# Two long-convolution filters moved to the start of a two-block forward pass, with a transform that pairs frequencies

## Chip, cores, metric

One core of one Trainium2 chip. The metric is the device time of one execution in microseconds (us). Before the change the median of 3 runs is 1393.35 us (1392.62 to 1395.66).

## What is computed

Two blocks over 256 tokens of width 1024. The first has two layers. Each layer modulates a normalized x by vectors made from a condition (`ada_w`), multiplies it by a wide `w_in`, and runs three branches: differential attention, a gated convolution ("hyena") and a gated MLP. In layer 0 a second stream, the context, goes through the same steps; in layer 1 it serves as keys and values only. The second block is a sparse attention and a feed-forward part; the change does not touch it.

The hyena branch convolves `u = x1 * v` with a filter of the sequence's length. The filter depends on weights alone, not on x:

```
z    = [t, cos(bands*wpos), -sin(bands*wpos)]              # 256 x 33
hid  = sin(freq0 * (z   @ w1 + b1))                        # 256 x 64
hid  = sin(freq1 * (hid @ w2 + b2))                        # 256 x 64
h    = (hid @ w3).reshape(256, 2, 512) * exp(-t*deltas)    # forward and backward half
k    = concat(h[:, 0], 0, reversed h[1:, 1]) / norm
y    = irfft(rfft(u) * rfft(k))[:256] + u * bias
```

The kernel does not use an FFT. It multiplies by cosine and sine matrices at 256 odd half-frequencies: `eo[.,0]` (sum of both halves) with cosines gives `Kc`, `eo[.,1]` (difference) with sines gives `Ks`, and the squared sums give the norm `rr`.

## The kernel before, in words

One class, `Body`, emits the program; `run` makes the pools, `block1` and `block2` emit the blocks. Each weight chunk of 512 KB is loaded by SyncE's queue (SP) into a `raw` buffer (3 of them), rounded by ScalarE to `hi` (L81), and VectorE makes the residue `lo` (L82): `unit`. TensorE then does three products per tile, hi with the high part of x, hi with its low part, lo with the high part (L61). Products of the filter are plain fp32 and show as two instructions each.

`block1` starts with the modulation of layer 0: four `mod_chunk` calls, each with two loads of 1 MB, fp32 products, two small transposing products and a few VectorE steps that end in `modA`. x and the context are loaded, normalized, transposed by TensorE (L735), modulated (L741, L743) and split into `hTh` and `hTl`. As soon as a pair of 128-row blocks of `hT` is there, its part of the first product X1 runs; four such steps interleave with `mod_chunk` 1 to 3. Then come packB (constants) and `filter_load(0)`.

The loop over the layers calls `hyena_in` (the rest of X1, then HV and X0, each four units of weights per layer), `hyena_filter`, `hyena_core` (the convolution by `K`), `gmlp`, the attention and the three gated branches. In layer 0 both the load and the computing of the filter come in that order, and its first hidden layer is the only part that reaches the startup. In layer 1 `filter_load(1)` stands right ahead of `hyena_filter`.

`hyena_filter` has two hidden layers (a small product, L401, six VectorE steps of `sin_red`, a sine on ScalarE at L261), then for each half of the 256 times two expansions by `w3`, five VectorE steps (L412 to L418) and two squares, then 16 small instructions for the norm and 8 products by `CS` that ScalarE copies to `K` (L433).

The order on each engine's queue is not the program's order as it stands. A planner replays the program when it is built, with the priority of program order, estimated durations and the number of free buffers, and writes each engine's queue; on the chip a queue runs strictly in order and waits where an input is late. SP's queue holds all loads, and a load waits there for its buffer.

Buffers that matter here: `slab` (8 KB per partition, 10 of them, shared by almost every large tile), `tf` (3 scratch tiles of 2 KB), 4 PSUM banks `pm` for all products but the large ones, 4 banks `pg` for those, and `x1` (the output of block 1, unused until the end of layer 0).

Of the kernel before, what the change touches and what calls it, by code (L numbers as in the profile page):

```python
# [7 lines left out]
F32 = mybir.dt.float32  # L8
# [23 lines left out]
class Body:  # L32
# [9 lines left out]

    def pool(self, name, bufs, psum=False, ctx=None):
        kw = dict(space=PSUM) if psum else {}
        return (ctx or self.ctx).enter_context(self.tc.tile_pool(name=name, bufs=bufs, **kw))
# [323 lines left out]

    def filter_load(self, l):  # L370
        nc = self.nc
        f = self.filt
        s1, s2, s3, s4 = [self.slab(f"f{i}").rearrange("p a b -> p (a b)") for i in range(4)]
        w3 = s1[:64, 0:1024]
        sqs = s1[:, 1024:2048].rearrange("p (t c) -> p t c", t=2)
        eo = s2.rearrange("p (t i c) -> p t i c", t=2, i=2)
        CS = s3[:, 0:1024].rearrange("p (t i f) -> p t i f", t=2, i=2)
        dec = s3[:, 1024:2048].rearrange("p (t c) -> p t c", t=2)
        zT = s4[:33, 0:256]
        hs = [s4[:64, 256:512], s4[:64, 512:768]]  # L380
        w1, w2 = s4[:33, 768:832], s4[:64, 832:896]
        nc.sync.dma_start(zT, self.a["zT"])
        nc.sync.dma_start(w1, self.a["hy_f_w1"][l])
        nc.sync.dma_start(w2, self.a["hy_f_w2"][l])
        nc.sync.dma_start(w3, self.a["hy_f_w3"][l])
        nc.sync.dma_start(CS, self.a["dft_k"])
        nc.sync.dma_start(dec, self.a["decay"])
        fc = f.tile([64, 4], F32, name=self.nm("ffc"), tag="ffc")
        nc.sync.dma_start(fc, self.a["hy_f_cols"][l])
        return w1, w2, w3, zT, hs, fc, eo, CS, dec, sqs  # L390

    def hyena_filter(self, l, ld):
        nc = self.nc
        f = self.filt
        w1, w2, w3, zT, hs, fc, eo, CS, dec, sqs = ld
        src = zT
        for i, w in enumerate((w1, w2)):
            ps = self.bank()[:64, :256]
            self.mm(ps, w, src)
            h = hs[i]  # L400
            nc.vector.tensor_scalar(h, ps, fc[:, i:i + 1], fc[:, 2 + i:3 + i], op0=OP.add, op1=OP.mult)  # L401
            self.sin_red(h, h, 256, p=64)
            src = h
        nps = self.bank()
        tcol = self.load_const("t0mask", [128, 2], pool=f)
        for t in range(2):
            h0 = self.bank()
            h1 = self.bank()
            self.mm(h0, src[:, t * 128:t * 128 + 128], w3[:, :512])
            self.mm(h1, src[:, t * 128:t * 128 + 128], w3[:, 512:])  # L410
            a0, a1 = self.tf(), self.tf()
            nc.vector.tensor_tensor(a0, h0, dec[:, t], op=OP.mult)  # L412
            nc.vector.scalar_tensor_tensor(a1, h1, tcol[:, t:t + 1], dec[:, t], op0=OP.mult, op1=OP.mult)
            nc.vector.tensor_tensor(eo[:, t, 0], a0, a1, op=OP.add)
            nc.vector.tensor_tensor(eo[:, t, 1], a0, a1, op=OP.subtract)
            nc.scalar.activation(a0, a0, AF.Square)
            nc.scalar.activation(a1, a1, AF.Square)
            nc.vector.tensor_tensor(sqs[:, t], a0, a1, op=OP.add)  # L418
        for c in range(4):
            for t in range(2):  # L420
                self.mm(nps[:, 2 * c:2 * c + 2], sqs[:, t, c * 128:c * 128 + 128], self.ones[:, :2], t == 0, t == 1)
        ssq = self.col(4, "hss")
        nc.vector.tensor_copy(ssq, nps[:, :8].rearrange("p (c i) -> p c i", i=2)[:, :, 0])
        rr = f.tile([128, 4], F32, name=self.nm("rr"), tag="rr")
        self.rpow(rr, ssq)
        nc.vector.tensor_scalar(rr, rr, 1.0 / 512.0, None, op0=OP.mult)
        K = self.slab("hyK")
        for i in range(2):
            for fi in range(2):
                ps = self.bank()  # L430
                for t in range(2):
                    self.mm(ps, CS[:, t, i, fi * 128:fi * 128 + 128], eo[:, t, i], t == 0, t == 1)
                nc.scalar.copy(K[:, 2 * i + fi], ps)  # L433
        return K, rr

# [265 lines left out]
    def block1(self, x1):  # L701
        nc, a = self.nc, self.a
        self.mc = [self.c1.tile([128, 24, 2], F32, name=f"mc{l}") for l in range(2)]
        self.A = [self.c1.tile([128, 8, 2], F32, name=f"modA{l}") for l in range(2)]
        self.load_pack("packA", PACK_A, self.const)
        c1 = self.cin
        self.cs = self.c1.tile([128, 8, 32], F32, name="cs")
# [4 lines left out]
        nc.vector.tensor_tensor(self.cs[:, :, 0:2], c1, th, op=OP.mult)  # L712
        self.mod_chunk(0, 0)
        xin = [a["x"], a["ctx"]]
        xs = []
        for s in range(2):
            t = self.slab("xs").rearrange("p a b -> p (a b)").rearrange("p (t d) -> p t d", t=2)
            nc.sync.dma_start(t, xin[s].rearrange("(t p) d -> p t d", p=128))
            xs.append(t)
        for s in range(2):  # L720
            for t in range(2):
                r = self.row_rstd(xs[s][:, t])
                nc.vector.tensor_scalar(xs[s][:, t], xs[s][:, t], r, None, op0=OP.mult)
        hTh = self.hT.tile([128, 8, 512], F32R, name="hTh0", tag="hTh")
        hTl = self.hT.tile([128, 8, 512], F32R, name="hTl0", tag="hTl")
        x1b = [self.gbank() for _ in range(4)]
        op0 = lambda k: (hTh[:, k], hTl[:, k])
        for ch in range(4):
            un = self.unit(a["w_in"][0][W1CH["X1"]][ch], 2)
            for k in (2 * ch, 2 * ch + 1):  # L730
                ps = self.bank()
# [23 lines left out]
        for l in range(2):  # L755
# [10 lines left out]
            u, x0 = self.hyena_in(l, nst, op, [(b, f, 1) for f, b in enumerate(x1b)] if l == 0 else None)  # L766
            K, rr = self.hyena_filter(l, fl if l == 0 else self.filter_load(l))
            if l == 1:
                self.pc = self.flat("packC")
                self.load_pack("packC", PACK_C, self.pc)  # L770
                self.rope_tables()
# [500 lines left out]
    def run(self):  # L1272
        nc, P = self.nc, self.pool
        self.const = P("const", 1)
        self.c1 = P("c1", 1)
        self.filt = P("filt", 1)
        self.cols = P("cols", 3)
        self.scr = P("scr", 2)
        self.att = P("att", 2)
        self.hT = P("hT", 1)  # L1280
        self.wraw, self.whi, self.wlo = P("wraw", 3), P("whi", 4), P("wlo", 4)
        self.slabs = P("slabs", 10)
        self.psg, self.psm = P("psg", 4, True), P("psm", 4, True)
        self.ones = self.const.tile([128, 128], F32, name="ones")
        nc.vector.memset(self.ones, 1.0)
        self.mhalf = self.const.tile([128, 1], F32, name="mhalf")
        nc.vector.memset(self.mhalf, -0.5)
        x1 = self.const.tile([128, 2, 1024], F32, name="x1")
        hTp = self.block1(x1)
        self.block2(x1, hTp)  # L1290


def prepare(inp):
    import numpy as np

# [28 lines left out]
    g = {k: np.asarray(v) for k, v in inp.items()}  # L1324
    o = {}
# [19 lines left out]
    hyb = c(cols(g["hy_bias"], 4).transpose(2, 0, 1))  # L1345
    o["hy_f_w1"] = c(g["hy_f_w1"])
    o["hy_f_w2"] = c(g["hy_f_w2"])
    o["hy_f_w3"] = c(g["hy_f_w3"])
    o["hy_f_cols"] = c(np.stack([g["hy_f_b1"], g["hy_f_b2"], g["hy_f_freq"][:, 0], g["hy_f_freq"][:, 1]], axis=-1))
    o["gm_ln_g"] = c(g["gm_ln_g"])  # L1350
# [14 lines left out]
    fi = g["w_ffn_in_2"][0]  # L1365
    fo = np.concatenate([np.concatenate([r(j * 256, j * 256 + 256), 2816 + r(j * 256, j * 256 + 256)]) for j in range(11)])
# [29 lines left out]
    rr = np.arange(128)  # L1396
# [10 lines left out]
    tt = np.arange(256)  # L1407
    fo = np.concatenate([np.arange(0, 256, 2), np.arange(1, 256, 2)]) + 0.5
    ang = 2 * np.pi * tt[:, None] * fo[None] / 512.0
    o["dft_k"] = c(np.stack([np.cos(ang), np.sin(ang)], axis=1).astype(f32).reshape(2, 128, 2, 256)  # L1410
                   .transpose(1, 0, 2, 3))
    fh = fo.reshape(2, 128)
# [13 lines left out]
    z = np.concatenate([t, np.cos(bands * wpos), -np.sin(bands * wpos)], axis=-1).astype(f32)  # L1426
    o["zT"] = c(z.T)
    deltas = np.abs(np.linspace(math.log(1e-2) / 1.5, math.log(1e-2) / 0.3, 512, dtype=f32))
    o["decay"] = c(np.exp(-t * deltas).astype(f32).reshape(2, 128, 512).transpose(1, 0, 2))
    m = np.ones((128, 2), f32)  # L1430
    m[0, 0] = 0.0
    o["t0mask"] = m
    loc = locals()
# [19 lines left out]
```

## Time and profile before

| | |
|---|---|
| median of 3 runs | 1393.35 us |
| profiled execution | 1392.87 us |
| its span, first to last instruction | 1390.9 us |
| granted TensorE clock over the span | 1.00 |

Times in the profile are microseconds from the first instruction. A row of a timeline gives start, duration, engine, line, operation, output and inputs by the program's names, shapes, a count of merged instructions, and in brackets the idle time of that engine just before with what ended it. A row of a stretch gives its length, then the busy time of each engine with its number of instructions, the granted clock (1.00 is 2.4 GHz), the mean busy share of the 16 DMA engines and what they moved in GB/s. TensorE is PE (matmul) and PEld (weight load), VectorE DVE, ScalarE ACT, GpSimd POOL, and SPq is SyncE's queue. `f` is the name of the old filter's tiles (its scratch apart), `pm` of a PSUM bank.

### The profile page before, as it was taken

To read this page: it belongs to the slowest core of one execution; us is meant where nothing else is said; L and a number is where in the kernel's file an instruction comes from. 1 tells how busy PE (TensorE), PEld (TensorE's weight loads), DVE (VectorE), ACT (ScalarE), POOL (GpSimd) and SP (SyncE) were. 2 spreads that over 40 slices of the span, in tenths; PEclk is the share of its full clock that TensorE was granted. 3 is DMA by queue.
4 is the path that set the end of the run, shared out by engine and by line. 5 is a ranking of instruction groups with operands and counts; after the bars stand their busy time and mean duration, and the time that the engine had idled before them with its cause. 6 is when DMAs were issued, how large, how long until landed. Compare 5 with 4: busy or idle time off the path is not lost.

```text
span 1390.9 us, 19805 instructions
## 1 busy us (share of the span) xinstructions
PE 1355.7 (97%) x7721; PEld 1134.1 (82%) x7721; DVE 897.1 (64%) x1574; ACT 621.5 (45%) x1046; POOL 43.3 (3%) x55
## 2 busy tenths in 40 slices
PE   6999999999999999999999999999999999999998
PEld 3786888777888888788688899987878897899996
DVE  3757842685388977388856755667776567655545
ACT  3532432564332334375535644554554645444433
POOL 0000000000000000010000000001002000000000
PEclk9999999999999999999999999999999999999999
DMA  9431222112535545327334255558315356665551
GB/s 388 143 107 61 81 89 92 63 46 67 201 111 191 220 178 183 136 92 234 107 96 135 93 171 187 182 165 289 122 57 160 103 173 193 207 204 191 184 182 46
DMA packets 55261, 206.22 MB, mean 148 GB/s; under 512 B 7102, under 2 KB 8320, under 8 KB 51584
## 3 DMA queue, kind: packets, MB, share of 16 engines
q1 hardware_dynamic: 55168, 204.95, 43.6%
q8 instruction: 61, 1.00, 0.3%
q14 instruction: 32, 0.26, 0.1%
HBM read 203.37 MB, written 1.05 MB: 147 GB/s over the span
## 4 chain that ended last, share of the span: by engine, by line
PE 83%; DVE 7%; DMA 4%; ACT 3%; issue 2%; POOL 1%; SPq 0%; POOLq 0%; ACTq 0%; DVEq 0%
PE pg L61 67%; PE pm L61 13%; DVE lo L82 1%; DMA ada<-ada_w 1%; PE pm L243 1%; DMA f<-hy_f_w 1%; DMA raw<-w_in 1%; ACT hi L81 1%; PE pm L614 1%; DMA xs<-x 1%; ACT p L603 1%; PE pm L947 1%; DVE hTl L67 1%; POOL rstd L145 0%; DVE mx L599 0%
## 5 line engine op out<-in xcount | busy, mean ns | idle before, releaser
L82 DVE TENSOR_TENSOR lo<-raw,hi 128x1024 fp32r<-128x1024 f32 (+1 forms) x242 | 293.6, 1215 | 246.2 <-ACT hi L81 245.1
L81 ACT CAST hi<-raw 128x1024 fp32r<-128x1024 f32 (+1 forms) x242 | 252.1, 1044 | 385.4 <-PE pg L61 332.5
L61 PE MATMUL pg<-hTh,hi 128*128 128x256 f32 (+1 forms) x920 | 305.0, 333 | 1.8 <-DMA f<-hy_f_w 1.4
L61 PE MATMUL pg<-hTl,hi 128*128 128x256 f32 (+1 forms) x920 | 305.2, 332 | 1.1 <-DVE hTl L67 1.1
L61 PE MATMUL pg<-hTh,lo 128*128 128x256 f32 (+1 forms) x920 | 303.9, 331 | 0.3 <-DVE lo L82 0.3
L61 PEld LDWEIGHTS pg<-hTh,hi 128*128 128x128 f32 x920 | 174.0, 189 | 24.5 <-issue 4.2
L61 PEld LDWEIGHTS pg<-hTl,hi 128*128 128x128 f32 x920 | 174.2, 189 | 21.0 <-issue 4.3
L61 PEld LDWEIGHTS pg<-hTh,lo 128*128 128x128 f32 x920 | 174.1, 189 | 18.5 <-issue 2.8
L61 PE MATMUL pg<-lo,hTh 128*128 128x512 f32 x400 | 158.7, 397 | 0.5 <-DVE lo L82 0.5
L61 PE MATMUL pg<-hi,hTh 128*128 128x512 f32 x400 | 158.9, 397 | 0.3 <-ACT hTh L66 0.2
L61 PE MATMUL pg<-hi,hTl 128*128 128x512 f32 x400 | 157.5, 394 | 1.0 <-DVE hTl L67 1.0
L82 DVE TENSOR_TENSOR wsl<-raw,wsl 128x1024 fp32r<-128x1024 f32 x66 | 80.2, 1223 | 70.1 <-ACT wsl L81 69.4
L61 PE MATMUL pg<-hTh,wsl 128*128 128x256 f32 x576 | 105.2, 284 | 0.0
L81 ACT CAST wsl<-raw 128x1024 fp32r<-128x1024 f32 x66 | 68.4, 1048 | 80.3 <-PE pg L61 50.3
L61 PEld LDWEIGHTS pg<-hTh,wsl 128*128 128x128 f32 x576 | 90.5, 192 | 0.3
L61 PEld LDWEIGHTS pg<-hi,hTl 128*128 128x128 f32 x400 | 75.2, 188 | 18.1 <-DVE hTl L67 1.9
L61 PEld LDWEIGHTS pg<-lo,hTh 128*128 128x128 f32 x400 | 75.3, 188 | 17.8 <-issue 2.5
L61 PEld LDWEIGHTS pg<-hi,hTh 128*128 128x128 f32 x400 | 75.2, 188 | 17.4 <-issue 1.5
L61 PE MATMUL pg<-hTl,wsl 128*128 128x256 f32 x288 | 81.7, 284 | 0.0
L61 PE MATMUL pg<-gh,lo 128*128 128x512 f32 (+1 forms) x192 | 64.8, 337 | 0.0
L61 PE MATMUL pg<-gh,hi 128*128 128x512 f32 (+1 forms) x192 | 64.7, 337 | 0.0
L61 PE MATMUL pg<-gl,hi 128*128 128x512 f32 (+1 forms) x192 | 64.6, 337 | 0.0
(363 smaller groups left out, 2031.8 us busy)
## 6 DMA issues: line engine op xcount, KB each, us to landing
raw<-w_in SPq DMA_DIRECT2D x172, 512.0 KB, 3.6
raw<-w_ffn_in SPq DMA_DIRECT2D x36, 512.0 KB, 3.6
ada<-ada_wT SPq DMA_DIRECT2D x16, 1024.0 KB, 6.8
raw<-w_branch SPq DMA_DIRECT2D x24, 512.0 KB, 3.5
raw<-w_out SPq DMA_DIRECT2D x24, 512.0 KB, 3.6
raw<-w_ffn_out SPq DMA_DIRECT2D x22, 512.0 KB, 4.0
ada<-ada_w SPq DMA_DIRECT2D x8, 1024.0 KB, 16.3
cw<-c_w SPq DMA_DIRECT2D x4, 1024.0 KB, 8.6
```

The source lines that it names most:

```text
L61: ins = self.nc.tensor.matmul(out, l, r, start=start, stop=stop)
L67: self.nc.vector.tensor_tensor(lo, src, hi.bitcast(F32), op=OP.subtract)
L81: nc.scalar.copy(hi, raw)
L82: nc.vector.tensor_tensor(lo, raw, hi.bitcast(F32), op=OP.subtract)
L243: nc.tensor.transpose(ps[:, k], src[:, k * 128:k * 128 + 128], self.ident)
L603: nc.scalar.activation(p[:, m, :KN], sb[m][:, :KN], AF.Exp, bias=nb[:, m:m + 1], scale=0.125, accum_out=ss[:, m:m + 1])
L614: nc.tensor.transpose(tp[:, k], w[:, k * 128:k * 128 + 128], self.ident)
L947: nc.tensor.transpose(tp[:, m, k], p[:, m, k * 128:k * 128 + 128], self.ident)
```

## The change

Both filters are emitted ahead of the layer loop. The small weights of both layers (`f_small`, 64 x 520 values) are loaded right after packA, the `w3` of both layers (64 x 2048) and the matrices with the decay (`f_dft`, 128 x 1538) after the first `mod_chunk`, ahead of x. Layer 0's `hyena_filter` stands between the normalization of x and the X1 product, layer 1's after packB. `eo` lives in `x1`, the other scratch in one slab. Layer 0's `K` has a tile of its own; layer 1's is a slab, written to DRAM and read back into layer 0's tile inside layer 1. The three loads take the place of seven per layer.

The transform uses that frequencies f and 256 − f have the same cosines at even times and opposite ones at odd times (sines the other way round). The times are therefore reordered on the host into even and odd halves; each half is multiplied once by the 128 low frequencies, and `K` for the low and the mirrored frequencies is the sum and the difference of both products. The slabs become 11, and the DMA scratch of the build is set to 256.

```diff
+    def filter_small(self):
+        t = self.scr.tile([64, 520], F32, name="fsmall", tag="ay", bufs=1)
+        self.nc.sync.dma_start(t, self.a["f_small"])
...
+    def filter_load(self):
+        nc = self.nc
+        s1, s2, self.fx = self.flat("f0"), self.flat("f1"), self.flat("f2")
+        nc.sync.dma_start(s1[:64].rearrange("p (l c) -> p l c", l=2), self.a["f_w3"])
...
+        nc.sync.dma_start(s2[:, :1538], self.a["f_dft"])
...
+        for i in range(2):
+            pe, po = self.bank(), self.bank()
+            self.mm(pe, self.fCS[:, 0, i], eo[:, 0, i])
+            self.mm(po, self.fCS[:, 1, i], eo[:, 1, i])
+            e = self.tf()
+            nc.scalar.copy(e, pe)
+            nc.vector.tensor_tensor(K[:, 2 * i], po, e, op=OP.add)
+            if i:
+                nc.vector.tensor_tensor(K[:, 2 * i + 1], po, e, op=OP.subtract)
+            else:
+                nc.vector.tensor_tensor(K[:, 2 * i + 1], e, po, op=OP.subtract)
...
-        K = self.slab("hyK")
-        for i in range(2):
-            for fi in range(2):
-                ps = self.bank()
-                for t in range(2):
-                    self.mm(ps, CS[:, t, i, fi * 128:fi * 128 + 128], eo[:, t, i], t == 0, t == 1)
-                nc.scalar.copy(K[:, 2 * i + fi], ps)
...
         self.load_pack("packA", PACK_A, self.const)
+        self.filter_small()
...
         self.mod_chunk(0, 0)
+        self.filter_load()
...
+        K = self.const.tile([128, 4, 512], F32, name="hyK")
+        eo = x1.rearrange("p t (i c) -> p t i c", i=2)
+        rrs = [self.hyena_filter(0, K, eo)]
         hTh = self.hT.tile([128, 8, 512], F32R, name="hTh0", tag="hTh")
...
         self.load_pack("packB", PACK_B, self.c1)
-        fl = self.filter_load(0)
+        K1 = self.slab("hyK1")
+        rrs.append(self.hyena_filter(1, K1, eo))
+        kd = self.pool("spill", 1, DRAM).tile([128, 2048], F32, name="kd")
+        nc.sync.dma_start(kd, K1.rearrange("p a b -> p (a b)"))
...
-            K, rr = self.hyena_filter(l, fl if l == 0 else self.filter_load(l))
+            rr = rrs[l]
             if l == 1:
+                nc.sync.dma_start(K.rearrange("p a b -> p (a b)"), kd)
                 self.pc = self.flat("packC")
...
-        self.slabs = P("slabs", 10)
+        self.slabs = P("slabs", 11)
```

## Rows read from the trace of the kernel before

**Rows 1.** The page's busy table: engine, busy us, share, instructions.
```profile
PE 1355.7 (97%) x7721; PEld 1134.1 (82%) x7721; DVE 897.1 (64%) x1574; ACT 621.5 (45%) x1046; POOL 43.3 (3%) x55
```

**Rows 2.** The chain of waits in order of time: start us, us, what.
```profile
2.10 9.23 DMA xs<-x
...
49.25 54.71 PE pg L61 x240
```

**Rows 3.** Stretches, all instructions.
```profile
0.00:25.07 25.07, 13.48 (x48) 4.14 (x48) 8.64 (x21) 10.15 (x23) 2.39 (x8) 1.00 0.94 376
25.07:49.25 24.18, 22.34 (x133) 14.74 (x131) 10.25 (x21) 6.89 (x11) 0.00 (x0) 1.00 0.74 269
49.25:103.89 54.64, 54.64 (x240) 44.95 (x240) 35.09 (x50) 23.93 (x30) 0.00 (x0) 1.00 0.36 115
...
638.00:677.00 39.00, 38.06 (x177) 27.24 (x175) 28.69 (x51) 17.76 (x25) 1.02 (x1) 1.00 0.59 196
```

**Rows 4.** Stretches, instructions on the filter tiles `f` alone: PE, PEld, DVE, ACT.
```profile
100.00:130.00 30.00, 13.16 (x42) 6.44 (x42) 7.99 (x13) 0.41 (x1) 1.00 0.26 88
638.00:677.00 39.00, 13.77 (x44) 6.59 (x44) 9.21 (x16) 0.83 (x2) 1.00 0.59 196
```

**Rows 5.** Timeline of TensorE around both filters.
```profile
48.29 0.64 PE L61 MATMUL pm<-f 33*64 33x256 f32 x2
...
111.73 3.70 PE L61 MATMUL pm<-f,f 64*128 64x512 f32 x8
...
118.17 4.54 PE L61 MATMUL pm<-f,f 128*128 128x512 f32 x10
...
124.02 2.82 PE L61 MATMUL pm<-f,f 128*128 128x512 f32 x6
...
644.35 0.61 PE L61 MATMUL pm<-f 33*64 33x256 f32 x2 [0.87 <-DMA f<-hy_f_w]
```

**Rows 6.** Timeline of VectorE and ScalarE in layer 0's filter.
```profile
52.88 0.53 DVE L401 TENSOR_SCALAR f<-pm,ffc 64x256 f32<-64x256 f32 x1
...
55.44 0.28 DVE L260 TENSOR_SCALAR tf<-tf 64x256 f32<-64x256 f32 x1
...
61.28 1.28 ACT L261 ACT_TABLE_LOAD   x1
62.57 0.42 ACT L261 ACTIVATE f<-tf 64x256 f32<-64x256 f32 x1
...
112.89 0.69 DVE L412 TENSOR_TENSOR tf<-pm,f 128x512 f32<-128x512 f32 x1 [0.33 <-PE pm L61]
...
121.22 0.69 DVE L418 TENSOR_TENSOR f<-tf,tf 128x512 f32<-128x512 f32 x1 [0.68 <-ACT tf L417]
...
142.93 0.69 DVE L514 TENSOR_TENSOR tf<-pm,hyK 128x512 f32<-128x512 f32 x1
```

**Rows 7.** Timeline of SP's queue: start us, us to issue.
```profile
22.48 0.37 SPq L382 DMA_DIRECT2D f<-zT  x1
...
57.25 0.43 SPq L865 DMA_DIRECT2D pos<-pos  x1
```

**Rows 8.** Stretches of the startup, all instructions.
```profile
10.00:20.00 10.00, 5.41 (x20) 2.83 (x16) 4.91 (x11) 6.61 (x17) 1.81 (x4) 1.00 1.02 426
20.00:30.00 10.00, 9.80 (x46) 4.19 (x45) 4.06 (x8) 3.09 (x5) 0.39 (x1) 1.00 1.02 429
...
36.00:38.00 2.00, 0.62 (x2) 0.30 (x2) 2.00 (x4) 1.48 (x3) 0.00 (x0) 1.00 0.95 302
```

**Rows 9.** Timeline of TensorE in the startup.
```profile
6.38 1.94 PE L61 MATMUL pm<-ada,cs 128*32 128x512 f32 x8 [6.38 <-DMA ada<-ada_w]
...
25.07 0.19 PEld L61 LDWEIGHTS pg<-hTh,hi 128*128 128x128 f32 x1 [1.32 <-ACT hTh L66]
...
28.50 1.06 PE L61 MATMUL pm<-ada,cs 128*32 128x512 f32 x8
```

More of the change, by code (lines that the diff above doesn't have):

```diff
@@ L14 @@
 PSUM = bass.MemoryType.PSUM
+DRAM = bass.MemoryType.DRAM
 EPS = 1e-6
@@ L41, in nm, with pool @@
         return f"{s}_{self.n}"
-    def pool(self, name, bufs, psum=False, ctx=None):
-        kw = dict(space=PSUM) if psum else {}
+    def pool(self, name, bufs, space=None, ctx=None):
+        kw = dict(space=space) if space else {}
         return (ctx or self.ctx).enter_context(self.tc.tile_pool(name=name, bufs=bufs, **kw))
@@ L368, in gg_tile @@
             nc.scalar.copy(g[:, n * 512:n * 512 + 512], ps)
-    def filter_load(self, l):
-        nc = self.nc
[L372 to L390, printed above, removed]
@@ L392, in hyena_filter @@
-    def hyena_filter(self, l, ld):
+    def filter_small(self):
+        t = self.scr.tile([64, 520], F32, name="fsmall", tag="ay", bufs=1)
+        self.nc.sync.dma_start(t, self.a["f_small"])
+        self.fz = t[:33, 0:256]
+        self.fw = [(t[:33, 256 + 64 * l:320 + 64 * l], t[:64, 384 + 64 * l:448 + 64 * l]) for l in range(2)]
+        self.fc = [t[:, 512 + 4 * l:516 + 4 * l] for l in range(2)]
+    def filter_load(self):
+        nc = self.nc
+        s1, s2, self.fx = self.flat("f0"), self.flat("f1"), self.flat("f2")
+        nc.sync.dma_start(s1[:64].rearrange("p (l c) -> p l c", l=2), self.a["f_w3"])
+        self.fw3 = [s1[:64, 1024 * l:1024 * l + 1024] for l in range(2)]
+        nc.sync.dma_start(s2[:, :1538], self.a["f_dft"])
+        self.fCS = s2[:, 0:512].rearrange("p (t i f) -> p t i f", t=2, i=2)
+        self.fdec = s2[:, 512:1536].rearrange("p (t c) -> p t c", t=2)
+        self.fm = s2[:, 1536:1538]
@@ L393, in hyena_filter @@
+    def hyena_filter(self, l, K, eo):
         nc = self.nc
[L394 to L397, printed above, removed]
+        fc = self.fc[l]
+        src = self.fz
+        sqs = self.fx[:, 0:1024].rearrange("p (t c) -> p t c", t=2)
+        for i, w in enumerate(self.fw[l]):
             ps = self.bank()[:64, :256]
             self.mm(ps, w, src)
-            h = hs[i]
+            h = self.fx[:64, 1024 + 256 * i:1280 + 256 * i]
@@ L403, in hyena_filter @@
             src = h
-        nps = self.bank()
-        tcol = self.load_const("t0mask", [128, 2], pool=f)
         for t in range(2):
[L407 to L410, printed above, removed]
+            h0, h1 = self.bank(), self.bank()
+            self.mm(h0, src[:, t * 128:t * 128 + 128], self.fw3[l][:, :512])
+            self.mm(h1, src[:, t * 128:t * 128 + 128], self.fw3[l][:, 512:])
             a0, a1 = self.tf(), self.tf()
-            nc.vector.tensor_tensor(a0, h0, dec[:, t], op=OP.mult)
-            nc.vector.scalar_tensor_tensor(a1, h1, tcol[:, t:t + 1], dec[:, t], op0=OP.mult, op1=OP.mult)
+            nc.vector.tensor_tensor(a0, h0, self.fdec[:, t], op=OP.mult)
+            nc.vector.scalar_tensor_tensor(a1, h1, self.fm[:, t:t + 1], self.fdec[:, t], op0=OP.mult, op1=OP.mult)
             nc.vector.tensor_tensor(eo[:, t, 0], a0, a1, op=OP.add)
@@ L418, in hyena_filter @@
             nc.vector.tensor_tensor(sqs[:, t], a0, a1, op=OP.add)
+        for i in range(2):
[9 more added lines that the diff above has]
+                nc.vector.tensor_tensor(K[:, 2 * i + 1], e, po, op=OP.subtract)
+        nps = self.bank()
         for c in range(4):
@@ L423, in hyena_filter @@
         nc.vector.tensor_copy(ssq, nps[:, :8].rearrange("p (c i) -> p c i", i=2)[:, :, 0])
-        rr = f.tile([128, 4], F32, name=self.nm("rr"), tag="rr")
+        rr = self.filt.tile([128, 4], F32, name=self.nm("rr"), tag=f"rr{l}")
         self.rpow(rr, ssq)
         nc.vector.tensor_scalar(rr, rr, 1.0 / 512.0, None, op0=OP.mult)
-        K = self.slab("hyK")
-        for i in range(2):
-            for fi in range(2):
-                ps = self.bank()
-                for t in range(2):
-                    self.mm(ps, CS[:, t, i, fi * 128:fi * 128 + 128], eo[:, t, i], t == 0, t == 1)
-                nc.scalar.copy(K[:, 2 * i + fi], ps)
-        return K, rr
+        return rr
     def slab(self, name, dt=F32):
@@ L1281, in run @@
         self.wraw, self.whi, self.wlo = P("wraw", 3), P("whi", 4), P("wlo", 4)
-        self.slabs = P("slabs", 10)
-        self.psg, self.psm = P("psg", 4, True), P("psm", 4, True)
+        self.slabs = P("slabs", 11)
+        self.psg, self.psm = P("psg", 4, PSUM), P("psm", 4, PSUM)
         self.ones = self.const.tile([128, 128], F32, name="ones")
@@ L1345, in prepare @@
     hyb = c(cols(g["hy_bias"], 4).transpose(2, 0, 1))
[L1346 to L1349, printed above, removed]
+    o["f_w3"] = c(g["hy_f_w3"].transpose(1, 0, 2))
+    fcols = np.stack([g["hy_f_b1"], g["hy_f_b2"], g["hy_f_freq"][:, 0], g["hy_f_freq"][:, 1]], axis=-1)
     o["gm_ln_g"] = c(g["gm_ln_g"])
@@ L1407, in prepare @@
     tt = np.arange(256)
[L1408 to L1411, printed above, removed]
+    tp = np.concatenate([tt[0::2], tt[1::2]])
+    fl = np.arange(0, 256, 2) + 0.5
+    fo = np.concatenate([fl, 256 - fl])
+    ang = 2 * np.pi * tp[:, None] * fl[None] / 512.0
+    dft = np.stack([np.cos(ang), np.sin(ang)], axis=1).astype(f32).reshape(2, 128, 256).transpose(1, 0, 2)
     fh = fo.reshape(2, 128)
@@ L1426, in prepare @@
     z = np.concatenate([t, np.cos(bands * wpos), -np.sin(bands * wpos)], axis=-1).astype(f32)
-    o["zT"] = c(z.T)
+    sm = np.zeros((64, 520), f32)
+    sm[:33, :256] = z.T[:, tp]
+    for l in range(2):
+        sm[:33, 256 + 64 * l:320 + 64 * l] = g["hy_f_w1"][l]
+        sm[:, 384 + 64 * l:448 + 64 * l] = g["hy_f_w2"][l]
+        sm[:, 512 + 4 * l:516 + 4 * l] = fcols[l]
+    o["f_small"] = sm
     deltas = np.abs(np.linspace(math.log(1e-2) / 1.5, math.log(1e-2) / 0.3, 512, dtype=f32))
-    o["decay"] = c(np.exp(-t * deltas).astype(f32).reshape(2, 128, 512).transpose(1, 0, 2))
+    dec = np.exp(-t * deltas).astype(f32)[tp].reshape(2, 128, 512).transpose(1, 0, 2)
     m = np.ones((128, 2), f32)
     m[0, 0] = 0.0
-    o["t0mask"] = m
+    o["f_dft"] = c(np.concatenate([dft.reshape(128, 512), dec.reshape(128, 1024), m], axis=1).astype(f32))
     loc = locals()
@@ L1445 @@
     arrays = prepare(inputs)
-    nc = bacc.Bacc("TRN2", target_bir_lowering=False, num_devices=1)
+    nc = bacc.Bacc("TRN2", target_bir_lowering=False, num_devices=1, dynamic_dma_scratch_size=256)
     aps = {n: nc.dram_tensor(n, v.shape, mybir.dt.from_np(v.dtype), kind="ExternalInput").ap() for n, v in arrays.items()}
```

## The prediction, made before the changed kernel was seen

> **What bounds the kernel now.** I read the busy table first. TensorE is busy 1355.7 of 1390.9 us, VectorE 897.1 [rows 1]: 35.2 us of TensorE's span are idle. Then the chain of waits: it begins with transfers, the first of them x, and from 49.25 us on it is TensorE in one unbroken piece of 240 matmuls in 54.71 us, 0.228 us each [rows 2]. The stretches say where the idle time is: in the first 25.07 us TensorE is busy 13.48, so 11.6 of its 35.2 idle us lie there, while the DMA engines are busy 94% of it; up to 49.25 us it idles another 1.8; from 49.25 to 103.89 us it does not idle at all, and in the stretch of layer 1's filter it idles 0.9 of 39.00 us [rows 3]. So from 25 us on the kernel is bound by TensorE, and before that by what has to be loaded. A filter instruction on TensorE costs its full time after 25 us and may be free before it.
>
> **What the filters cost now.** The stretches of the filter tiles alone give TensorE 13.16 us between 100 and 130 us and 13.77 us between 638 and 677 [rows 4]; layer 0's first hidden layer stands apart, 0.64 us at 48.29 [rows 5]. That is 13.80 and 13.77 us for the two layers, 27.6 in all, none of it before 25 us. In layer 1 TensorE also idles 0.87 us for the filter's own weights [rows 5], nearly all of the idle time of that stretch. Both go: −28.5 us at TensorE's end.
>
> **The new transform.** Of a layer's 13.8 us the cosine and sine products take 10 + 6 instructions in 4.54 + 2.82 = 7.36 us [rows 5], which is 8 products of two instructions each. The change makes 4 products (even and odd times are multiplied once by the low frequencies; sum and difference give the low and the mirrored high ones), so 3.7 us. The hidden layers, the expansions and the squared sums stay. A layer's filter is then 13.8 − 3.7 = 10.1 us of TensorE. Instead of four ScalarE copies per layer there are two copies and four VectorE additions with one PSUM operand; the nearest row is L412 with 0.69 us [rows 6], so 2.8 us of VectorE per layer.
>
> **Layer 0's filter in the startup.** Its loads are three: 130 KB and 512 KB on 64 partitions, 769 KB on 128, 1.445 MB, and in the program all three stand ahead of x. They replace seven loads, which today are issued from 22.48 us on, behind the modulation weights [rows 7]. The DMA engines are full until 38 us [rows 8], so what stands ahead pushes what stands behind. At the 426 GB/s of 10 to 20 us that is 3.4 us; at the 302 GB/s of 36 to 38 us, when the old 64-row weights were landing and the engines were 95% busy, it is 4.8 us [rows 8]. I take the slow rate for the 64-row part (0.657 MB, 2.2 us) and the fast one for the rest (0.787 MB, 1.8 us): 4.0 us.
>
> The Trainium skill ("SBUF — State Buffer", section "Door 1: The DMA port swizzle") says that a tile on 64 partitions reaches only half of the memory's DMA ports and loads about as slowly as one on 32. By that rule at half of 426 GB/s the term would be 4.9 instead of 4.0 us. The trace agrees in direction: busy engines, fewer bytes, just in the slices with such loads.
>
> On TensorE the 10.1 us have to fit ahead of the first X1 matmul, now at 25.07 us [rows 9]. With x 4 us later the window up to there has 25.07 + 4 − 13.48 = 15.6 idle us, of which I leave 4 for the small weights to land (the 1 MB of modulation weights next in the queue is used at 6.38 us [rows 9]): 11.6 us for 10.1. It fits, but as a chain. A hidden layer is 0.6 us of matmul, the VectorE steps from 52.88 to 55.72 us (2.84 us) and a sine of 0.42 us, once with a table load of 1.28 us [rows 6]; two of them end near 13 us. From the first expansion (111.73) to the last squares (121.91) it is 10.2 us today [rows 5, 6]; so 23 us, and products and sums are done near 28. The first X1 matmul waits for the transposed x (hTh [rows 9]), which then comes at about 29 us. I add 2 us for last products and VectorE steps that fall in front of it. Startup: +6 us. Bounds: 3.4 (loads alone at the fast rate) and 4.0 + 10.1 = 14.1 (nothing hidden).
>
> **Layer 1's filter.** In the program it stands behind the X1 product and packB. After X1's start TensorE is full, so it costs 10.1 us again. If its hidden layers and expansions (3.70 us [rows 5] and 1.2) slip into the startup it costs 5.2. I take 10.1. A layer's VectorE work is 2 × 2.84 for the hidden layers, ten steps of about 0.69 from L412 to L418 and the 2.8 from above, 15.4 us [rows 6]. For the second there are 13.9 idle VectorE us between 25.07 and 49.25 us and 19.6 up to 103.89 [rows 3], so I count the work itself at nothing, and 1 us for filter steps that stand in VectorE's queue ahead of a transposed x or a weight residue on which TensorE waits (bounds 0, and eight steps of 0.69 us = 5.5).
>
> **The trip through DRAM.** 1.05 MB are written and read back on SP's queue. The write waits for K1, and behind it in program order stand the loads of the HV and X0 weights. Three raw buffers are loaded ahead, each feeding 24 matmuls or 5.5 us [rows 2], so SP may stand 16 us before TensorE sees it. The read-back waits for that write and for layer 0's last read of K at 142.93 us [rows 6], and is wanted near 650 us. Loads of layer 1 are pulled forward by the planner that orders the instructions (layer 1's `pos` load is issued at 57.25 us, in the middle of layer 0 [rows 7]), so I expect it there as well. The DMA share is 0.36 from 49 to 104 us and 0.59 from 638 to 677, with the old filter loads still in it [rows 3]. Cost 0; bounds 0 and 2.5 us each way (1.05 MB at 426 GB/s).
>
> Removed with layer 1's filter is also its VectorE and ScalarE work beside TensorE. I count no gain for it, as TensorE is the engine that is late there. The 11th slab buffer, fewer slabs held across layer 0 and the smaller DMA scratch add no instruction: 0.
>
> **Sum.** −28.5 + 10.1 + 6 + 1 = −11.4 us. The profiled execution took 1392.87 us with a span of 1390.9; 1392.87 − 11.4 = 1381.5. It lies 0.5 us under the median of the runs, inside their scatter, so I leave it at 1381.5.
>
> **Rivals.**
> 1. *More is hidden.* Layer 1's hidden layers and expansions run in the startup too, the loads go at the fast rate, no VectorE stalls: −28.5 + 5.2 + 3.4 = −19.9, 1373.0 us. For it: its inputs are loaded with layer 0's. Against: both share buffers, and VectorE's idle time before 25.07 us is 16.4 us [rows 3], about one filter's work.
> 2. *The early matmuls run slowly.* Eight modulation instructions take 1.94 us at 6.38 and 1.06 us at 28.50 [rows 9], 1.83 times, although the granted clock reads 1.00 (2.4 GHz) in every stretch [rows 3, 8]; before the first eight TensorE had done nothing, while from 20 to 30 us it is busy 9.80 of 10 [rows 8]. At that rate layer 0's filter is 18.5 us, 8.4 more, and the startup grows to 14.4: −28.5 + 10.1 + 14.4 + 1 = −3.0, 1389.9 us. Against: the added work itself keeps TensorE busy. The Trainium skill ("TensorE: Matmul & The Clock Gate", "Part 1: The HAM clock gate") has such a rule: the array starts at half rate and is released by activity. By it the durations agree and the column of granted clock does not.
> 3. *Not done in the startup.* The planner starts X1 first, and both filters come behind it: −28.5 + 20.2 + 3.4 = −4.9, 1388.0 us; only the shorter transform is left as a gain. For it: today layer 0's first hidden layer is through TensorE at 48.93 us [rows 5], and its VectorE steps begin at 52.88 [rows 6], after the transposed x. Against: in the program the filter stands ahead of X1.
> 4. *Slower: both filters ahead of X1, one behind the other, at the slow rate.* Per filter: hidden layers 2 × (1.1 + 2.84 + 0.42) = 8.8, expansions to squares 10.2 + 0.83 × 3.7 = 13.3, products 3.7 × 1.83 = 6.8; 28.9 us. Two end at 4 + 57.8 = 61.8 us, X1 starts 36.7 us late, and the sum is −28.5 + 36.7 = +8.2, 1401.1 us. It decides from a first X1 matmul later than 25.07 + 28.5 = 53.6 us. Against: in the program X1 stands ahead of layer 1's filter.
>
> **How the numbers follow.** Forecast 0.48, rival 1 0.17, rival 2 0.13, rival 3 0.14, rival 4 0.08. The forecast's own range is 1376 to 1387. For 8 in 10 I take 1372 to 1390.5: it takes in rivals 1 and 3 and most of 2, and leaves out rival 4, half of what lies under rival 1 and the upper part of rival 2. A change under 0.2% (2.8 us) can't be told from none. Faster by more (below 1390.6): forecast, rivals 1 and 3 and half of 2, less a little for weights that the new order of instructions may bring late, 0.84. Within: 0.08. Slower: 0.08.
>
> **What would show it.** The first X1 matmul between 28 and 32 us; the instructions of the filter tiles on TensorE about 10 us per layer; layer 0's before that matmul, layer 1's between it and 100 us; no filter instruction and no filter load between 600 and 700 us, and the read-back issued before 600 us. The stretch from layer 1's X0 product to its attention is some 14 us shorter. Wrong: a first X1 matmul after 36 us (rivals 2 and 4), a VectorE idle reason of TensorE that sums to several us before 60 us, SP standing on K1 while ScalarE waits for weights, or a gain in layer 1 well under 14 us.

## The result and the profile after

The changed kernel takes 1409.27 us (median of 4 runs, 1407.85 to 1414.39) where the kernel before takes 1393.17 beside it. The ratio is 1.0119, 95% interval [1.0091, 1.0147]: 16 us slower, not 12 us faster. The profiled execution took 1409.39 us with a span of 1407.5, 16.6 more than before.

The busy table of the changed kernel, engine by engine as in [rows 1]:

```profile
PE 1356.8 (96%) x7705; PEld 1135.2 (81%) x7705; DVE 902.9 (64%) x1582; ACT 619.3 (44%) x1042; POOL 45.1 (3%) x55
```

TensorE's idle time grew from 35.2 to 50.7 us, 15.5 of the 16.6. Its busy time rose by 1.1 although 16 instructions went: the two filters took 16.8 and 17.0 us of TensorE instead of 13.8 each. TensorE's timeline of the startup, changed kernel (start, duration, idle time before in brackets):

```profile
12.73 1.87 PE L62 MATMUL pm<-packA,th 128*128 128x2 f32 x8 [0.81 <-DVE th L340]
14.53 1.11 PE L62 MATMUL pm<-fsmall 33*64 33x256 f32 x2
20.18 1.11 PE L62 MATMUL pm<-f,fsmall 64*64 64x256 f32 x2 [4.54 <-ACT f L262]
29.23 7.19 PE L62 MATMUL pm<-f,f 64*128 64x512 f32 x8 [7.93 <-ACT f L262]
36.35 2.07 PE L62 MATMUL pm<-x,f 128*128 128x512 f32 x2
38.67 3.63 PE L62 MATMUL pm<-x,f 128*128 128x512 f32 x6 [0.25 <-DVE x L407]
42.15 0.28 PE L62 MATMUL pm<-ones,f 128*128 128x2 f32 x2
42.29 0.64 PE L738 MATMUL pm<-packA,xs 128*128 128x128 f32 x4
...
46.83 0.96 PE L62 MATMUL pg<-hTh,hi 128*128 128x512 f32 x3
```

The first X1 matmul comes at 46.83 us instead of 25.07 [rows 9]. The reader is to see that all 36 instructions of layer 0's filter but the last 14 stand ahead of the first transposes of x (L738), that TensorE idles 4.54 and 7.93 us in the middle of them, and that the eight expansions take 7.19 us where the old ones took 3.70 [rows 5]. In the kernel before, the first transposes came right behind the first normalized block:

```profile
15.34 0.69 PE L735 MATMUL pm<-packA,xs 128*128 128x128 f32 x2 [2.00 <-DVE xs L723]
```

VectorE around the second hidden layer, changed kernel:

```profile
21.66 0.53 DVE L397 TENSOR_SCALAR f<-pm,fsmall 64x256 f32<-64x256 f32 x1
22.41 0.75 DVE L723 TENSOR_SCALAR xs<-xs,rstd 128x1024 f32<-128x1024 f32 x1 [0.23 <-POOL rstd L146]
23.08 0.28 DVE L256 TENSOR_SCALAR tf<-f 64x256 f32<-64x256 f32 x1
...
27.78 0.75 DVE L723 TENSOR_SCALAR xs<-xs,rstd 128x1024 f32<-128x1024 f32 x1 [0.45 <-POOL rstd L146]
28.45 0.28 DVE L261 TENSOR_SCALAR tf<-tf 64x256 f32<-64x256 f32 x1
```

x and the context are normalized by 28.5 us (L723; the first of four blocks by 20.1) and could be transposed then; the transposes wait until 42.29 behind the filter. The seven VectorE steps of a hidden layer, which in the kernel before took the first one 2.84 us without a break (52.88 to 55.72, [rows 6], from L401 on), are spread from 21.66 to 28.73 for the second one, between those of the normalization.

The second loss stands between X1 and HV. TensorE, then ScalarE, then the stretches there (busy time of PE, PEld, DVE, ACT, POOL with instructions, then granted clock, DMA share, GB/s):

```profile
79.73 0.64 PE L62 MATMUL pm<-f,fsmall 64*64 64x256 f32 x2
84.78 7.19 PE L62 MATMUL pm<-f,f 64*128 64x512 f32 x8 [4.41 <-ACT f L262]
...
98.96 1.84 PE L62 MATMUL pm<-ones,f 128*128 128x2 f32 x16
101.81 0.76 PE L62 MATMUL pg<-hTh,hi 128*128 128x512 f32 x1 [1.00 <-DVE hyX L453]
```

```profile
94.87 0.63 ACT L409 ACTIVATE tf<-tf 128x512 f32<-128x512 f32 x1 [0.28 <-DVE x L408]
95.41 0.61 ACT L410 ACTIVATE tf<-tf 128x512 f32<-128x512 f32 x1
95.93 1.43 ACT L448 ACTIVATE hyX<-pg,packB 128x512 f32<-128x512 f32 x2
```

```profile
80.00:90.00 10.00, 5.59 (x8) 2.16 (x7) 5.75 (x12) 1.07 (x2) 0.00 (x0) 0.73 0.17 52
90.00:100.00 10.00, 9.68 (x22) 3.91 (x20) 7.33 (x13) 6.06 (x10) 0.00 (x0) 0.58 0.00 0
...
79.73:101.81 22.08, 16.35 (x36) 7.01 (x35) 14.42 (x25) 7.50 (x12) 0.73 (x1) 0.69 0.10 35
```

X1's last matmul ends at 79.7 and HV's first comes at 101.81. In between TensorE has nothing but the last 34 of the 36 instructions of layer 1's filter (the row counts one matmul of X1 and one of HV at its edges), at a mean granted clock of 0.69. HV needs the four banks `pg` that hold X1. They are freed by X1's short convolutions, three steps per bank that read X1 out of PSUM (L448 on ScalarE, L451 and L453 on VectorE). The first L448 starts at 95.93, right behind the filter's squares (L409, L410) in ScalarE's queue, and the first L453 ends at 101.66, after which HV's first matmul starts. In the kernel before, the same last step on the first bank ended at 60.03, as X1 was ending:

```profile
59.29 0.74 DVE L455 SCALAR_TENSOR_TENSOR hyX<-pg,packB,hyX 128x510 f32<-128x510 f32 x1
```

In the changed kernel ScalarE is busy 1.07 of 10 us from 80 to 90: it isn't loaded, it waits in order.

What came back later shows at layer 1's HV. ScalarE's reads of the HV banks in the kernel before and in the changed one (minimum, median and maximum in ns, then first and last start in us; the last is in layer 1), and the filter tiles of the changed one from 600 to 700 us:

```profile
L450 ACT ACTIVATE hyHV<-pg,packB x8: 557/674/781, 78.2 to 637.2; 128x512 f32<-128x512 f32 x4, 128x256 f32<-128x256 f32 x4
```

```profile
L448 ACT ACTIVATE hyHV<-pg,packB x8: 553/673/782, 121.4 to 667.1; 128x512 f32<-128x512 f32 x4, 128x256 f32<-128x256 f32 x4
```

```profile
600.00:700.00 100.00, 0.00 (x0) 0.00 (x0) 0.00 (x0) 0.00 (x0) 1.00 0.49 158
```

| from | to | before | after | difference |
|---|---|---|---|---|
| start | first X1 matmul | 25.1 | 46.8 | +21.8 |
| first X1 matmul | end of X1 | 35.0 | 32.9 | −2.2 |
| end of X1 | first HV matmul | 0 | 22.1 | +22.1 |
| first HV matmul | layer 1's HV read | 577.1 | 565.3 | −11.8 |
| layer 1's HV read | end of the span | 753.7 | 740.4 | −13.3 |

(X1 is 96 matmuls; before, the 96th starts at 60.05 us and HV follows at once. Differences are taken before rounding.) The removed filters gave back 25.1 us (the two last rows). The two new places cost 41.7 (the three first).

### The profile page after: what moved, and what is told of

The parts are those of the page before. It is cut to its first block, busy times and chain, and to the rows that moved or that the text cites. A ratio compares the mean times of both kernels' runs of the same rounds, so it can differ in the third digit from the quotient of the medians.

```text
span 1407.5 us, 19757 instructions
## 1 busy us (share of the span) xinstructions
PE 1356.8 (96%) x7705; PEld 1135.2 (81%) x7705; DVE 902.9 (64%) x1582; ACT 619.3 (44%) x1042; POOL 45.1 (3%) x55
## 4 chain that ended last, share of the span: by engine, by line
PE 81%; DVE 9%; ACT 4%; DMA 3%; issue 2%; POOL 1%; SPq 0%; POOLq 0%; ACTq 0%; DVEq 0%
PE pg L62 65%; PE pm L62 13%; DVE lo L83 2%; PE pm L244 1%; DMA xs<-x 1%; ACT hi L82 1%; ACT p L601 1%; PE pm L612 1%; DVE mx L597 1%; DMA raw<-w_in 1%; DMA raw<-w_ffn_in 1%; DVE hTl L68 1%; PE pm L954 1%; POOL rstd L146 1%; DVE wsl L83 1%
## 5 line engine op out<-in xcount | busy, mean ns | idle before, releaser
L62 PEld LDWEIGHTS pg<-hi,hTh 128*128 128x128 f32 x400 | 75.2, 188 | 16.6 <-issue 1.1
```

What stands on the lines that cost most here:

```text
L62: ins = self.nc.tensor.matmul(out, l, r, start=start, stop=stop)
```

## Experiments

Each run is timed beside the kernel before on its chip; the ratios are to that, and differences in us are worked out from them on the scale of 1393.2 us. A difference between two runs is known only to 4 to 6 us, since both ratios have an interval; what moved where is read from the traces.

**The transform alone.** In the kernel before, with the filters where they were:

```diff
-                ps = self.bank()
-                for t in range(2):
-                    self.mm(ps, CS[:, t, i, fi * 128:fi * 128 + 128], eo[:, t, i], t == 0, t == 1)
...
+            self.mm(pe, CS[:, 0, i], eo[:, 0, i])
+            self.mm(po, CS[:, 1, i], eo[:, 1, i])
```

> The kernel before with the paired transform alone; both filters are loaded and computed where they were. Theory A (the loss comes from where the filters stand in the queues, the transform is the gain it was counted as): TensorE loses 3.7 us per layer, 1393.2 - 7.4 = 1386 us, the first X1 matmul stays at 25 us. Rival B (the pairing itself costs: its VectorE additions or its PSUM banks hold TensorE up): 1391 us or more, with TensorE waiting on the additions.

Ratio 0.9969 [0.9952, 0.9986], −4.3 us (−6.7 to −2.0). TensorE on the filter tiles (PE, PEld, DVE, ACT):

```profile
0.00:200.00 200.00, 10.42 (x36) 5.16 (x36) 9.21 (x16) 0.83 (x2) 0.99 0.42 145
600.00:700.00 100.00, 10.65 (x36) 5.15 (x36) 9.20 (x16) 0.83 (x2) 1.00 0.50 155
```

A filter at full rate is 10.42 and 10.65 us instead of 13.80 and 13.77: 6.5 saved, not the 7.4 of theory A. TensorE waits for none of the additions, so rival B's cause is not there. The time lies between both, and its interval just holds the 6.5. Behind layer 1's filter TensorE has two waits that the kernel before doesn't have, 1.12 us for a rounded weight (`hi`, L81) and 0.56 us for a step of the gated MLP (`gmu`, L653); with them 4.8 of the 6.5 would be left. Why they arise was not tested.

**Which filter, and where.** In the changed kernel the filters were moved behind layer 0's `hyena_in`: layer 1's, layer 0's, both.

```diff
             u, x0 = self.hyena_in(l, nst, op, ...)
+            if l == 0:
+                K1 = self.slab("hyK1")
+                rrs.append(self.hyena_filter(1, K1, eo))
```

> The changed kernel with layer 1's filter (and its write to DRAM) emitted behind layer 0's X0 product instead of ahead of the layer loop; layer 0's filter stays ahead of X1. Theory A: X1's short convolutions no longer stand behind that filter in ScalarE's and VectorE's queues, HV follows X1 within 1 us instead of 22 us later, the filter costs about 10 us at the full rate behind X0: 1409.3 - 22 + 10 = 1397 us. Rival C (HV waits because packB, which the short convolutions read, comes late): HV still starts more than 10 us after X1 ends, 1406 us or more.

Ratio 1.0017 [0.9997, 1.0036], 14 us under the changed kernel. X1 still begins at 46.90. All of TensorE, then the filter tiles (PE, PEld, DVE, ACT):

```profile
80.00:90.00 10.00, 10.00 (x46) 8.29 (x45) 4.78 (x6) 2.46 (x3) 0.00 (x0) 1.00 0.30 89
```

```profile
110.00:185.00 75.00, 9.81 (x34) 4.93 (x34) 5.47 (x9) 0.41 (x1) 1.00 0.31 100
```

TensorE is full where it had waited, and the same filter costs 9.81 + 0.64 us. packB arrives as before, so rival C falls.

> The changed kernel with layer 0's filter emitted behind layer 0's X0 product; its loads stay ahead of x, and layer 1's filter stays ahead of the layer loop. Theory A: X1 starts at about 30 us (25 plus 4 to 6 for the loads ahead of x) instead of 46.8, and the filter costs 10 us at the full rate later: 1409.3 - 17 + 10 = 1402 us. Rival D (it is the three loads ahead of x, and not the computing, that delay X1): X1 stays later than 40 us, about 1419 us.

Ratio 1.0092 [1.0061, 1.0122], 3.8 us under the changed kernel instead of 7.

```profile
29.67 0.50 PE L62 MATMUL pg<-hTh,hi 128*128 128x512 f32 x1
...
65.00 0.64 PE L62 MATMUL pm<-f,fsmall 64*64 64x256 f32 x2
...
87.78 0.76 PE L62 MATMUL pg<-hTh,hi 128*128 128x512 f32 x1 [1.00 <-DVE hyX L453]
```

X1 begins at 29.67, so the loads ahead of x cost 4.6 us and the filter the other 17.2 of 21.8; rival D falls. The gap of 22 us ahead of HV is the old one. I had counted 17 us of gain, but HV came only 14.0 earlier (87.78 against 101.81): X1's stretch became 2.4 us longer, 1.5 of it idle TensorE time (1.45 in one wait for the transposed x at 42 us, which the changed kernel doesn't have), and the gap 0.7. With 10.5 for the filter that is 3.5, near the 3.8; but the intervals of both ratios overlap, so the time alone shows no gain.

> The changed kernel with both filters emitted behind layer 0's X0 product; the loads stay ahead of x, the trip through DRAM stays. Theory A: both gains add, 1409.3 - 12 - 7 = 1390 us; the same from the other side: 1393.2 - 7.4 (transform) - 0.9 (layer 1's wait for its load) + 4 to 6 (loads ahead of x) = 1389 to 1391. Rival D: X1 later than 40 us, 1405 us or more.

Far from theory A, and like rival D in time alone: ratio 1.0115 [1.0084, 1.0145]. X1 begins at 29.78 and HV follows X1, but a new hole opens after X0:

```profile
142.64 0.64 PE L62 MATMUL pm<-f,fsmall 64*64 64x256 f32 x2
...
147.91 6.06 PE L62 MATMUL pm<-f,f 64*128 64x512 f32 x8 [3.04 <-ACT f L262]
```

```profile
140.00:150.00 10.00, 6.96 (x24) 4.13 (x24) 6.15 (x13) 1.88 (x3) 0.00 (x0) 0.95 0.32 104
150.00:160.00 10.00, 9.69 (x12) 3.20 (x11) 6.92 (x11) 3.02 (x6) 0.00 (x0) 0.53 0.01 2
```

```profile
159.86 0.59 ACT L417 COPY tf<-pm 128x512 f32<-128x512 f32 x1 [1.85 <-PE pm L62]
...
168.01 0.60 ACT L644 ACTIVATE gv<-pg 128x512 f32<-128x512 f32 x1
```

The second filter again stands alone on TensorE, its expansions in 6.06 us (granted clock 0.53 from 150 to 160). GV's last product, in the four `pg` banks, ends before 145 us. Its first read, the gelu of the gated MLP (L644), comes at 168.01, behind this filter and the convolution's copies in ScalarE's queue, and the next product into those banks (GU) at 174.54. It is the picture of X1 and HV at another place; that the late reads hold GU here is read from the order of the rows and was not tested by a run of its own.

**What holds HV.** X1's short convolutions emitted ahead of layer 1's filter, nothing else:

```diff
+        s0 = self.slab("hyX1")
+        for f, b in enumerate(x1b):
+            self.short(b, 0, 4 + f, s0[:, f], 2)
         K1 = self.slab("hyK1")
         rrs.append(self.hyena_filter(1, K1, eo))
```

> The changed kernel with X1's four short convolutions emitted ahead of layer 1's filter; the filter itself stays ahead of HV in the program, layer 0's filter ahead of X1. Theory J (HV waited 22 us because the four PSUM banks of X1 were held by short convolutions standing behind the filter's steps in ScalarE's and VectorE's queues): HV starts within 2 us of X1's end, the filter's matmuls fall between HV's at the full rate, about 10.4 us; 1409.3 - 22 + 10.4 = 1397.5 us, as with the filter behind X0. Rival K (a filter emitted ahead of HV delays HV by its own chain, whatever holds the banks): HV starts more than 10 us after X1's end, 1405 us or more.

Ratio 1.0009 [0.9994, 1.0025], 1394.5 us on the scale, 15 us under the changed kernel. (The median itself, 1397.58 us, looks like theory J's 1397.5, but the kernel before took 1396.99 beside it.) Theory J's 11.6 us of gain lies inside what is known of the difference; rival K's 4 does not. All work, then the filter tiles:

```profile
90.00:100.00 10.00, 10.00 (x41) 6.11 (x39) 7.36 (x12) 3.48 (x6) 0.00 (x0) 1.00 0.18 54
```

```profile
90.00:100.00 10.00, 6.96 (x27) 3.48 (x25) 3.64 (x6) 0.00 (x0) 1.00 0.18 54
```

The filter is at about the same place in time (its expansions start at 88.23 us) and TensorE is full around it: HV's matmuls fill its waits. So the short convolutions behind the filter held the banks; a filter emitted ahead of HV does not open the gap by itself.

**The rate in the startup.** Extra products on TensorE (constants into banks that nobody reads) behind the hidden layers of layer 0's filter, first 6 and 12, then 9 and 20:

```diff
             src = h
+            for _ in range((6, 12)[i] if l == 0 else 0):
+                self.mm(self.bank()[:, :256], self.ones, self.cs.rearrange("p k c -> p (k c)"))
```

> The changed kernel with 18 extra products (constants into unused PSUM banks, read by nobody) on TensorE in the startup, 6 behind the first and 12 behind the second hidden layer of layer 0's filter, where TensorE waits 4.5 and 7.9 us for the sines. Theory E (the filter's matmuls run at half rate there because TensorE stood idle before them): the 8 expansion instructions take 3.7 instead of 7.2 us, the 8 products 3.7 instead of 5.7, X1 starts 5 to 6 us earlier, near 41 us, and the total is 5 us under the changed kernel, about 1404 us. Rival F (they are slow for another cause, such as the loads that keep the DMA engines full until 40 us or the 64-row operands): the 8 expansions stay at 7 us and X1 starts at 47 us or later.

Ratio 1.0117 [1.0067, 1.0166], X1 at 48.30. Timeline, and the stretch of the expansions:

```profile
21.39 5.64 PE L62 MATMUL pm<-cs,ones 128*128 128x256 f32 x24
29.87 7.19 PE L62 MATMUL pm<-f,f 64*128 64x512 f32 x8 [2.84 <-ACT f L262]
```

```profile
30.00:37.00 7.00, 7.00 (x9) 2.37 (x9) 3.35 (x6) 1.15 (x2) 0.00 (x0) 0.50 1.01 414
```

By its own words rival F wins here, but the rows say otherwise: the 24 extra products behind the second layer ran at 0.235 us an instruction, then TensorE stood 2.84 us, and the expansions took 7.19 at a granted clock of 0.50, 1.2 GHz. The gap had to be closed before one could decide.

> As the run with 18 extra products in the startup, but with 9 behind the first and 20 behind the second hidden layer of layer 0's filter, so that the 2.8 us gap that was left ahead of the expansions is filled. Theory E (that gap brought the low rate back: in the earlier run the products behind the hidden layers took 0.235 us per instruction, the expansions after the gap 0.9 at a granted clock of 0.50): the 8 expansion instructions take 3.7 to 4 us, the products about 4, X1 starts at 41 to 43 us instead of 46.8, about 1404 us. Rival F (the 64-row operands or the loads beside them): 7.2 us again at a granted clock of 1.00, X1 at 47 us or later.

```profile
24.34 8.90 PE L62 MATMUL pm<-cs,ones 128*128 128x256 f32 x40
33.18 3.70 PE L62 MATMUL pm<-f,f 64*128 64x512 f32 x8
...
40.82 5.49 PE L62 MATMUL pm<-x,f 128*128 128x512 f32 x6 [2.89 <-DVE x L409]
```

```profile
32.00:36.00 4.00, 4.00 (x13) 2.13 (x12) 1.46 (x3) 0.00 (x0) 0.00 (x0) 1.00 1.01 419
```

Without a gap the expansions take 3.70 us, as [rows 5], at a granted clock of 1.00 and with the DMA engines as full as in the run before (share 1.01 in both stretches); so it is TensorE's clock, not the operands or the loads. The Trainium skill ("TensorE: Matmul & The Clock Gate", "Part 1: The HAM clock gate") says that the throttled state is the default and that activity releases it; these runs agree, 7.19 us behind a wait and 3.70 behind work. The time was missed: X1 came at 54.55 and the ratio is 1.0121 [1.0096, 1.0147]. The extra products delayed the expansions by 4 us, and behind them TensorE waited 2.89 us for VectorE and fell to the low rate again. Filling the waits of this chain made its matmuls faster in one place and did not bring X1 earlier.

**The normalization of x as the cause of the long chain.** Layer 0's filter emitted ahead of it:

```diff
+        rrs = [self.hyena_filter(0, K, eo)]
         for s in range(2):
             for t in range(2):
                 r = self.row_rstd(xs[s][:, t])
...
-        rrs = [self.hyena_filter(0, K, eo)]
```

> The changed kernel with layer 0's filter emitted ahead of the normalization of x instead of behind it. Theory A2 (the chain of its hidden layers is long because its VectorE and ScalarE steps stand between those of the normalization): the two sines come 3 to 4 us earlier, X1 starts at 43 to 44 us, 1405 us. Rival H (the normalization is not what it waits for; the chain is set by the small modulation products ahead of it on TensorE and by the rate): X1 starts within 1 us of 46.8, 1408 to 1410 us.

Ratio 1.0100 [1.0068, 1.0132], X1 at 46.30.

```profile
20.30 1.11 PE L62 MATMUL pm<-f,fsmall 64*64 64x256 f32 x2 [4.59 <-ACT f L262]
28.00 7.19 PE L62 MATMUL pm<-f,f 64*128 64x512 f32 x8 [6.59 <-ACT f L262]
```

Only 0.5 us earlier, the number of rival H. But the order on VectorE's queue still alternates normalization and second hidden layer, so theory A2 was not put to the test, and what that interleaving costs by itself stays open.

**A better place.** In the changed kernel: loads behind packB, layer 0's filter behind `hyena_in`, layer 1's behind the gated MLP.

```diff
             yc = self.gmlp(l, tiles, op)
+            if l == 0:
+                K1 = self.slab("hyK1")
+                rrs.append(self.hyena_filter(1, K1, eo))
```

> The changed kernel with all three filter loads behind packB, layer 0's filter behind layer 0's X0 product and layer 1's filter behind layer 0's gated MLP; the paired transform and the trip through DRAM stay. Theory A: X1 starts at 25 us, HV follows X1 at once, no wait in layer 1 for its filter's loads; against the kernel before only the shorter transform (10.4 instead of 13.8 us per layer, as the first runs had it) and 0.9 us are left: 1393.2 - 6.8 - 0.9 = 1385.5 us. Rival G (layer 1's filter and the trip through DRAM cost something in layer 0 wherever they stand, by PSUM banks, VectorE's queue or SP's): 1391 us or more, with a TensorE wait or a low granted clock near the filter.

Ratio 0.9967 [0.9945, 0.9989]. Timed again:

> The kernel with the loads behind packB, layer 0's filter behind X0 and layer 1's behind the gated MLP once more, for a closer interval. Theory A: shorter transform and layer 1's load wait, 6.8 + 0.9 us under the kernel before, a ratio of 0.9945. Rival G: ratio 0.998 or above.

Ratio 0.9936 [0.9913, 0.9959]; median 1387.47 beside 1396.99. Up to the first X1 matmul, and where both filters lie:

```profile
0.00:24.44 24.44, 12.90 (x48) 3.32 (x49) 8.74 (x21) 10.17 (x23) 2.40 (x8) 0.79 0.93 372
100.00:200.00 100.00, 100.00 (x452) 74.13 (x450) 81.47 (x152) 42.02 (x69) 5.06 (x5) 1.00 0.23 72
```

It beats both kernels. X1 begins at 24.44, TensorE doesn't idle from 100 to 200 us, and each filter is 10.5 us of TensorE. Both intervals hold theory A's 0.9945, the first only at its edge, and the second leaves rival G's 0.998 out.

Last, the transform alone with layer 0's loads later:

```diff
-        fl = self.filter_load(0)
...
-            K, rr = self.hyena_filter(l, fl if l == 0 else self.filter_load(l))
+            K, rr = self.hyena_filter(l, self.filter_load(l))
```

> The kernel before with the paired transform and with layer 0's filter loads emitted right ahead of the filter instead of behind packB; on SP's queue they then stand behind the weights of HV and X0 instead of ahead of them. Theory A: the transform gives 6.8 us and the 1.45 us wait of X1 at 37 us, behind which the filter's loads stand, goes too: 1393.2 - 6.8 - 1.5 = 1385 us. Rival I (that wait is the modulation weights' or X1's own weights, not the filter's): the wait stays, 1386.5 us.

Ratio 0.9993 [0.9972, 1.0014], −1.0 us (−3.9 to +2.0): this missed both theory A (−8.3) and rival I (−6.8). On the wait rival I holds: it stays 1.45 us, now put down to another releaser, so it wasn't the filter's loads.

```profile
36.73 1.15 PE L61 MATMUL pg<-hTh,hi 128*128 128x512 f32 x2 [1.45 <-ACT hTh L66]
```

The trace has new waits besides: 1.29 us of TensorE for the filter's first sine at 114 us, 0.7 us more for the transposed x at 50 us, and the two behind layer 1's filter that the transform alone has too. So the later loads are no improvement, and how much of the transform's 6.5 us reaches the time is not settled by these two runs.

## Why the prediction was wrong

*What the filters cost (−28.5).* Right in kind, 25.1 us instead of 28.5: from layer 1's HV on the span is 13.3 us shorter, predicted some 14, and no filter work is left there. In layer 0 11.8 came back, of 13.2 on TensorE.

*The transform (−3.7 a layer).* Right for TensorE's work, mis-sized by a little: 3.4 and 3.1.

*The loads (+4.0, bounds 3.4 to 4.8).* Right as far as can be told: 4.6 with layer 0's filter moved away. (Three kernels with the loads behind x start X1 at 24.1 to 24.4 us instead of 25.07, so it may be up to 5.6.) The estimate by the rule of the Trainium skill ("SBUF — State Buffer", "Door 1: The DMA port swizzle") was 4.9; the measured value decides neither.

*"It fits, but as a chain" (startup +6, upper bound 14.1).* This step failed: +21.8, with the first X1 matmul at 46.83 us, past the 36 us that I had named as a sign of being wrong. I compared 11.6 idle TensorE us with 10.1 of work, and let X1 come when x was transposed, as if X1 could pass the filter. TensorE's queue has the filter first, so its waits for sines (12.5 us) hold x's transposes as well. "Nothing hidden" was no upper bound because it held busy time alone. Two smaller errors fed it: the first hidden product stood behind the modulation's small ones until 14.53 us, where I had both layers done by 13; and the filter was busy 16.8 us, not 10.1, at the low rate (rival 2's mechanism, which I had priced without the waits). Of the 17.2 us beyond the loads the rate is at most 6.4 (16.8 against 10.4 at the full rate); how much of the rest the interleaving on VectorE makes stays open.

*"After X1's start TensorE is full, so it costs 10.1 us" (layer 1's filter).* This failed too: 22.1 us. I looked in VectorE's queue for steps ahead of a transposed x or a weight residue, priced 1 us, and did not ask who frees the PSUM banks that the next product needs. Moving either the filter or the four short convolutions closed the gap and gave back 14 and 15 us.

*VectorE's steps ahead of X1's inputs (+1).* Not seen: X1's stretch became 2.2 us shorter, 1.5 of it idle TensorE time that is gone.

*The trip through DRAM (0).* Right: SyncE stood 18.1 us for the write and 13.2 for the read-back, which was issued at 167.66, far ahead of 600. During the second wait TensorE is busy 10.00 of every 10 us (110 to 170); the first, 82.4 to 100.6 us, lies in the gap ahead of HV, and TensorE is full from HV's start on. The kernel with the better place keeps the trip.

*Rivals.* Rival 4 had the sign and the low rate, but not the place: it put both filters ahead of X1, 36.7 us; it was one ahead of X1 and one ahead of HV. Rival 3's −4.9 is near what the better place gave (−4.6, then −8.9), but that is no point for it: in the changed kernel X1 did not start first, as it had assumed.

## To carry to other kernels

Idle time of an engine is not room for a chain: on a queue that runs in order each wait of the chain is paid by everything behind it (12.5 us here), so bound a moved chain from above by its full length, waits and low clock included. For every step moved ahead of a big product, ask who empties the PSUM banks that product writes, and whether those reads now stand behind the moved step. Emit side work where independent matmuls stand behind it, and emit the readers of the banks first.

## What the runs showed of the chip

The granted clock of a profile can read 1.00 while instructions take the time of the low level: the eight expansions of the changed kernel take 7.19 us in a startup of 1.00, and 7.19 again from 84.78 on, where the stretches around them read 0.73 and 0.58 and the one from 84.78 to 91.97 reads 0.50. The stretch of the startup:

```profile
28.00:36.00 8.00, 6.77 (x8) 2.50 (x8) 4.06 (x7) 1.26 (x3) 0.00 (x0) 1.00 1.02 420
```

The startup of the kernel with the better place reads 0.79 and the one before 1.00 [rows 3], although the first eight modulation matmuls take 1.94 us in both. The duration of equal instructions is the safer sign here. And in the run with 18 extra products a wait of 2.84 us between matmuls was followed by the low level at once.
